# One fixed order on TensorE for the matmuls and transposes of a layer's expert pairs

## Chip, core and metric

The kernel runs on one core of a Trainium2 chip. The metric is device time in microseconds (us). The median of three runs before the change is 1332.66 us (1327.23 to 1333.02); the profile below is of a further execution, which took 1326.95 us.

## What is computed

The reference is one step of a two-layer backbone over 512 latent tokens and 128 context tokens of width 1024. Each layer mixes tokens (attention, pooling, convolution) and then sends them through 16 experts. The expert part, which the change touches, is:

```
aff = softmax(u @ w_router)                  # per token, over 16 experts
g, idx = top_k(aff.T, cap)                   # cap = 64 latent tokens or 16 context tokens per expert
xs = u[idx]
hdn = silu(xs @ w_gate) * (xs @ w_up)        # 1024 -> 512
ye = (hdn @ w_down) * g                      # 512 -> 1024
out = zeros.at[idx].add(ye)
x = layer_norm(ALPHA * x + gate2 * out)
```

All of it is float32. The weights of one expert are 6 MB, so a layer reads 96 MB of them.

## The kernel before

`experts` runs the 16 experts as eight pairs, j = 0 to 7, in a loop that Python unrolls. The two experts of a pair share the 128 columns of TensorE: `lat` (L1129) computes gate and up for the latent rows with expert i in columns 64i to 64i+63, and `context` (L1137) does the same for the context rows with four products (two experts, gate and up) in 32 columns each. `lat_down` (L1187) and `ctx_down` (L1159) are the down projections, in two tiles of 64 columns and four of 32. `lat(0)` and `lat(1)` are the two halves of the contraction over 1024, `context(ks)` any of its eight steps k.

One f32 matmul leaves two MATMUL records in the profile, so a pair has 64 records of `ps_g` and `ps_u`, 64 of `ps_gc`, 32 of `ps_d` and 32 of `ps_dc`. Records on different column tiles that start together are called a round here: four records of a 32-column product or two of a 64-column product. A pair is thus 32 + 16 + 16 + 8 = 72 rounds. To these come 16 transposes: eight in `load_x` (via `transpose8`, L239), which turn the gathered rows of the next pair, four of `hT` (L1176, `lat_transpose`) and four of `hcT` (L1152, in `ctx_down`).

Between them stand the other engines. `lat_hidden` makes h = silu(ps_g) * ps_u (ScalarE L1167, VectorE L1169); `ctx_down` makes hc alike from `ps_gc` (L1145, L1147) and copies `ps_hcT` out (L1153); `lat_transpose` copies `ps_hT` out in two halves (L1177, L1178); `modulate` (L247, L250) scales each of `load_x`'s eight transposed blocks into `xT`, four to a PSUM bank, by turns on VectorE and ScalarE. GpSimd gathers the rows of the next pair (L947) and scatters the results into DRAM with two indirect DMAs each (L1094: `yacc` for latent rows, `yaccc` for context rows). SyncE issues the weight loads (L1062), twelve of 1 MB per pair, into 16 slots; a load into a slot waits until the matmuls that read the slot's last tile are done.

PSUM: `ptr` gives out two banks (`tr8`, `ps_hT`, and before the change `ps_hcT`), `pmisc` one, `ps_gu` three (`ps_g`, `ps_u`, `ps_gc`), `ps_dn` two (`ps_d`, `ps_dc`).

What decides the order: the program's order is a priority only. A list scheduler simulates the engines while the kernel is built and gives each engine the instruction that its model holds ready; a fixed edge between two instructions exists only where data or `tc.issue_after` makes one. So the order on TensorE of `lat`, `context`, `ctx_down` and the next pair's first matmuls, which depend on one another little, is what the model picks. Before the change the program's order for pairs 1 to 6 is `context(0..3)`, `lat(0)`, `lat(1)`, `context(4..7)`, hT, `load_x`, `lat_down`, `ctx_down`. Pair 0 fills the routing's waits with `context`. After pair 7 `join` adds the residual and the last pair's results in PSUM (`ps_z`, L1261 to L1266) and `finish` normalises each block of 128 tokens.

Of the kernel before, what the change touches and what calls it, by code (L numbers as in the profile page):

```python
# [21 lines left out]
P = 128  # L22
D = 1024
TL = 512
# [3 lines left out]
KD = 8  # L28
# [16 lines left out]
NPAIR = NE // 2  # L45
# [20 lines left out]
def kernel(ctx: ExitStack, tc: tile.TileContext, a: dict):  # L66
# [44 lines left out]
    def ptr(name):  # L111
        return ps_t.tile([P, 512], F32, tag="tr", name=name)
# [118 lines left out]
        nc.tensor.matmul(out, lhsT=lh, rhs=rl, start=False, stop=False)  # L231
        nc.tensor.matmul(out, lhsT=ll, rhs=rh, start=False, stop=last)  # L232

    def transpose8(src, emit, psum=ptr):

        for g in range(2):
            ps = psum("tr8").rearrange("p (k n) -> p k n", k=4)
            for kk in range(4):
                ins = nc.tensor.transpose(ps[:, kk, :], src[:, 512 * g + kk:512 * g + 512:4], ident)  # L239
            emit(g, ps)  # L240
        return ins

# [799 lines left out]
    def experts(l, A, B, ctxr, ln, gates, newrow, newhalf, residual, xc, route_late, ps_dn, preload, start_next, finish, keep):  # L1042
        wk = opool(f"moe{l}", "right")
        ex = [opool(f"exp{i}_{l}", "right") for i in range(NEX)]
        ps_gu = Banks(f"gu{l}", 3)
        nslot, paced = [0], []

        def eload(src, shape, name):

# [34 lines left out]
        def load_x(j):  # L1084
            x = gather(newrow("xsl"), zrow[:, :], lgi[:, j:j + 1]) if j else x_first
            xT = xp.tile([P, KD, P], F32, tag="xT", name="xT", bufs=2)
            transpose8(x, lambda g, ps: modulate(xT[:, 4 * g:4 * g + 4], ps, A, B, 0, g))
            return xT

        def scatter(acc, y, idx, j):  # L1090
# [15 lines left out]
        for j in range(NPAIR):  # L1106
# [18 lines left out]
            def lat(hf):  # L1125
                for ps, nm in ((pg, "g"), (pu, "u")):
                    for k in range(4 * hf, 4 * hf + 4):
                        for i in range(2):
                            nc.tensor.matmul(ps[64 * i:64 * i + 64, :], lhsT=xT[:, k, 64 * i:64 * i + 64],  # L1129
                                             rhs=w[nm, i, hf][:, k % 4, :], start=(k == 0), stop=(k == KD - 1))  # L1130

            def context(ks):

                for k in ks:
                    for q in range(4):
                        i, nm = q // 2, "gu"[q % 2]
                        ins = nc.tensor.matmul(pc[32 * q:32 * q + 32, :], lhsT=xc[:, k, 16 * es[i]:16 * es[i] + 32],  # L1137
                                               rhs=w[nm, i, k // 4][:, k % 4, :], start=(k == 0), stop=(k == KD - 1))
                return ins

            def ctx_down(pd=None, after=None):
                sc = newhalf("sc")
                hc = newhalf("hc")[0:64]
                for i in range(2):
                    nc.scalar.activation(out=sc[64 * i + 32:64 * i + 64], in_=pc[64 * i:64 * i + 32], func=AF.Silu)  # L1145
                    with tc.issue_after(after.ins) if after else ExitStack():
                        nc.vector.tensor_tensor(out=hc[32 * i:32 * i + 32], in0=pc[64 * i + 32:64 * i + 64],  # L1147
                                                in1=sc[64 * i + 32:64 * i + 64], op=ALU.mult)
                hcT = wk.tile([P, 4, 64], F32, tag="hcT", name="hcT", bufs=1)
                pt = ptr("ps_hcT")[:, 0:256].rearrange("p (k n) -> p k n", k=4)  # L1150
                for k in range(4):
                    nc.tensor.transpose(pt[:, k, :], hc[:, 256 * (k // 2) + k % 2:256 * (k // 2) + 256:2], ident[0:64, 0:64])  # L1152
                nc.scalar.copy(out=hcT, in_=pt)  # L1153
                if pd is None:
                    pd = ps_dn.tile("ps_dc")
                for f in range(4):
                    for q in range(4):
                        i, n = q // 2, q % 2
                        nc.tensor.matmul(pd[32 * q:32 * q + 32, :], lhsT=hcT[:, f, 32 * i:32 * i + 32],  # L1159
                                         rhs=w["d", i, f // 2][:, f % 2, n * 512:n * 512 + 512], start=(f == 0), stop=(f == 3))  # L1160
                yc = newhalf("yc") if j == NPAIR - 1 else wk.tile([P, 512], F32, tag="yc", name="yc", bufs=2)
                nc.vector.scalar_tensor_tensor(out=yc, in0=pd, scalar=cg[:, j:j + 1], in1=gc2, op0=ALU.mult, op1=ALU.mult)  # L1162
                return yc

            def lat_hidden():
                sg = newhalf("sg")
                nc.scalar.activation(out=sg, in_=pg, func=AF.Silu)  # L1167
                h = newhalf("h")
                nc.vector.tensor_tensor(out=h, in0=pu, in1=sg, op=ALU.mult)  # L1169
                return h  # L1170

            def lat_transpose(h):
                hT = wk.tile([P, 4, P], F32, tag="hT", name="hT", bufs=1)
                pt = ptr("ps_hT").rearrange("p (k n) -> p k n", k=4)
                for k in range(4):
                    nc.tensor.transpose(pt[:, k, :], h[:, 256 * (k // 2) + k % 2:256 * (k // 2) + 256:2], ident)  # L1176
                nc.scalar.copy(out=hT[:, 0:2], in_=pt[:, 0:2])  # L1177
                nc.vector.tensor_copy(out=hT[:, 2:4], in_=pt[:, 2:4])  # L1178
                return hT

            def lat_down(hT):
                ye = newrow("ye")
                for n in range(2):
                    pd = ps_dn.tile("ps_d")
                    for f in range(4):
                        for i in range(2):
                            nc.tensor.matmul(pd[64 * i:64 * i + 64, :], lhsT=hT[:, f, 64 * i:64 * i + 64],  # L1187
                                             rhs=w["d", i, f // 2][:, f % 2, n * 512:n * 512 + 512], start=(f == 0), stop=(f == 3))
                    hs = slice(n * 512, n * 512 + 512)
                    order["ye"] = nc.vector.scalar_tensor_tensor(out=ye[:, hs], in0=pd, scalar=lg[:, j:j + 1], in1=gl2[:, hs], op0=ALU.mult, op1=ALU.mult)  # L1190
                return ye

            if j == 0:
                quads = list(range(KD))

                def fill(n, after=None):
                    ks = [quads.pop(0) for _ in range(min(n, len(quads)))]
                    with tc.issue_after(after.ins) if after else ExitStack():
                        return context(ks)

                (lgi, lso, lg, llast), x_first = route_late(fill)
                xp = opool(f"xT{l}", "left")
                scatter(yaccc, ctx_down(after=order["lgi"]), csi, j)
                x_next = load_x(0)
                for t in (1, 2, 3):
                    residual(t, order["last"].ins if t == 3 else None)
            xT = x_next
            if j == 0:
                lat(0)
                lat(1)  # L1210
            elif j < NPAIR - 1:
                context(range(4))
                lat(0)
                lat(1)
                context(range(4, 8))
            else:
                lat(0)
                lat(1)
                context(range(4))
            hT = lat_transpose(lat_hidden())  # L1220
            if j < NPAIR - 1:
                x_next = load_x(j + 1)
            ye = lat_down(hT)
            if j == MIDAT:
                order["mid"] = order["ye"]
            if j < NPAIR - 1:
                scatter(yacc, ye, lso, j)
                if j:
                    scatter(yaccc, ctx_down(), csi, j)


        z2 = []
# [6 lines left out]
                                    scalar2=None, op0=ALU.is_equal)  # L1239
        hotr = newhalf("hotr", F32R)  # L1240
        nc.vector.tensor_scalar(out=hotr, in0=iota, scalar1=llast[:, 0:1], scalar2=None, op0=ALU.is_equal)
        context(range(4, 8))
        yh, yl = gates.tile([P, D], F32R, tag="gate", name="yh"), newrow("yl", dt=F32R)
        for n in range(2):
            cols = slice(n * 512, n * 512 + 512)
# [9 lines left out]

        def join(t):
            res = []
            for n in range(2):
                ps = seats(t, n)
                cols = slice(n * 512, n * 512 + 512)  # L1260
                nc.tensor.matmul(ps, lhsT=ident, rhs=zs[t][:, cols], start=True, stop=False)  # L1261
                if t == CTX:
                    nc.tensor.matmul(ps, lhsT=hot[:, TL + n * P:TL + (n + 1) * P], rhs=yc, start=False, stop=True)
                else:
                    for y in (yh, yl):
                        nc.tensor.matmul(ps, lhsT=hotr[:, t * P:(t + 1) * P], rhs=y[:, cols], start=False, stop=y is yl)  # L1266
# [244 lines left out]
```

## Time and profile before

| | |
|---|---|
| median of three runs | 1332.66 us |
| the profiled execution | 1326.95 us, its span 1325.1 us |
| TensorE (PE) busy | 1237.7 us, 93% of the span |
| VectorE, ScalarE, GpSimd busy | 542.6, 370.7, 253.7 us |
| chain of work that ended last | PE 86%, DVE 7%, ACT 3%, DMA 2% |
| moved by DMA | 342.35 MB, 258 GB/s over the span |

The profile has one line per group of instructions or per stretch of time. PE is TensorE, DVE VectorE, ACT ScalarE, POOL GpSimd, SPq the queue of SyncE. PEclk is the granted share of TensorE's clock: 1.00 is the upper of its two levels (2.4 GHz). `L1129` is the line of the kernel; `ps_g<-wg,xT 128*64` is a matmul into `ps_g` from `wg` and `xT` on a tile of 128 rows and 64 columns. The chain of waits is read back from the last instruction: each piece is what the next one waited for.

### The profile page before, as it was taken

How to read it: one execution, taken by the hardware profiler on the slowest of the kernel's cores; microseconds unless marked ns; L12 is line 12 of the kernel's file. 1: busy time of each engine (PE TensorE's matmuls, PEld its weight loads, DVE VectorE, ACT ScalarE, POOL GpSimd, SP SyncE). 2: the span in 40 equal slices, each digit the busy share in tenths (PEclk: the TensorE clock that was granted, in tenths of full speed). 3: DMA queues.
4: the chain of work that ended last, by engine and by line, in shares of the span. 5: the costliest groups of instructions: out<-in, count | busy, mean ns of one | idle time of the engine just before them, and what ended most of it. 6: DMA issues, size and time to landing. Idle time of an engine off the chain costs nothing.

```text
span 1325.1 us, 18215 instructions
## 1 busy us (share of the span) xinstructions
PE 1237.7 (93%) x7244; PEld 716.4 (54%) x7244; DVE 542.6 (41%) x1266; ACT 370.7 (28%) x800; POOL 253.7 (19%) x234
## 2 busy tenths in 40 slices
PE   4999999999699999999978999999968999999994
PEld 1877786977333333233248998798743333333322
DVE  1554365776611121112196666577662111111216
ACT  1532145752321111011144423475341111101111
POOL 1210002005221220122166100200523122012204
PEclk8999999999899999999988999999999999999997
DMA  9868657065799999998442214606479999999831
GB/s 357 306 223 281 235 210 276 2 225 190 277 381 407 395 398 420 361 320 282 147 135 96 74 54 193 249 5 224 168 293 350 406 397 397 421 370 328 299 100 79
DMA packets 85078, 342.35 MB, mean 258 GB/s; under 512 B 18712, under 2 KB 32088, under 8 KB 54400
## 3 DMA queue, kind: packets, MB, share of 16 engines
q1 hardware_dynamic: 73568, 305.96, 59.5%
q0 software_dynamic: 9840, 29.45, 8.6%
q10 hardware_dynamic: 1584, 5.77, 1.1%
q8 instruction: 57, 0.93, 0.3%
q14 instruction: 29, 0.24, 0.1%
HBM read 313.73 MB, written 27.51 MB: 258 GB/s over the span
## 4 chain that ended last, share of the span: by engine, by line
PE 86%; DVE 7%; ACT 3%; DMA 2%; issue 1%; POOL 0%; SPq 0%; POOLq 0%; ACTq 0%; DVEq 0%
PE ps_gc L1137 10%; PE ps_d L1187 9%; PE ps_u L1129 9%; PE ps_g L1129 9%; PE ps_dc L1159 5%; PE ps_ada L185 4%; PE ps_c L230 3%; PE ps_c L232 3%; PE ps_c L231 3%; PE ps_o L231 3%; PE ps_o L230 3%; PE ps_o L232 3%; PE tr L239 2%; DMA r_wA<-in_w_in_dram 1%; PE ps_p L719 1%; PE ps_a L232 1%
## 5 line engine op out<-in xcount | busy, mean ns | idle before, releaser
L1129 PE MATMUL ps_u<-wu,xT 128*64 128x512 f32 x512 | 134.9, 595 | 0.0
L1137 PE MATMUL ps_gc<-wu,xc 128*32 128x512 f32 x512 | 134.0, 596 | 0.0
L1137 PE MATMUL ps_gc<-wg,xc 128*32 128x512 f32 x512 | 132.9, 596 | 0.0
L1129 PE MATMUL ps_g<-wg,xT 128*64 128x512 f32 x512 | 131.8, 597 | 0.1
L1187 PE MATMUL ps_d<-wd,hT 128*64 128x512 f32 x512 | 122.9, 598 | 3.5 <-ACT hT L1177 3.1
L1169 DVE TENSOR_TENSOR h<-ps_u,sg 128x512 f32<-128x512 f32 x16 | 11.1, 691 | 239.3 <-PE ps_u L1129 212.5
L1129 PEld LDWEIGHTS ps_u<-wu,xT 128*64 128x64 f32 x512 | 40.2, 137 | 82.4 <-issue 77.0
L1094 POOL DMA_INDIRECT yaccc<-yc,csi x28 | 39.8, 1423 | 216.6 <-DVE yc L1162 155.1
L1129 PEld LDWEIGHTS ps_g<-wg,xT 128*64 128x64 f32 x512 | 37.7, 136 | 79.7 <-issue 71.4
L1167 ACT ACTIVATE sg<-ps_g 128x512 f32<-128x512 f32 x16 | 9.5, 596 | 252.7 <-PE ps_g L1129 252.7
L1187 PEld LDWEIGHTS ps_d<-wd,hT 128*64 128x64 f32 x512 | 35.8, 136 | 70.0 <-issue 62.2
L1159 PE MATMUL ps_dc<-wd,hcT 128*32 128x512 f32 x512 | 67.3, 620 | 0.9 <-ACT hcT L1153 0.9
L185 PE MATMUL ps_ada<-wada,cs 128*32 128x512 f32 x368 | 58.8, 615 | 6.0 <-DMA wada<-in_w_ada_dram 6.0
L1137 PEld LDWEIGHTS ps_gc<-wg,xc 128*32 128x32 f32 x512 | 29.2, 109 | 51.7 <-issue 49.1
L1145 ACT ACTIVATE sc<-ps_gc 32x512 f32<-32x512 f32 x32 | 18.8, 588 | 129.5 <-PE ps_gc L1137 106.2
L247 ACT ACTIVATE xT<-tr,modB,modA 128x128 f32<-128x128 f32 x64 | 29.1, 458 | 85.7 <-DVE xT L250 85.3
L1162 DVE SCALAR_TENSOR_TENSOR yc<-ps_dc,cg,gc 128x512 f32<-128x512 f32 x16 | 12.0, 751 | 95.5 <-PE ps_dc L1159 85.4
L1137 PEld LDWEIGHTS ps_gc<-wu,xc 128*32 128x32 f32 x512 | 30.3, 109 | 37.4 <-issue 35.8
L250 DVE TENSOR_SCALAR xT<-tr,modA,modB 128x128 f32<-128x128 f32 x64 | 26.0, 408 | 57.0 <-PE tr L239 49.3
L947 POOL DMA_INDIRECT xsl<-zrow,lgi x16 | 15.9, 992 | 160.4 <-PE tr L239 146.1
L1190 DVE SCALAR_TENSOR_TENSOR ye<-ps_d,lg,gl 128x512 f32<-128x512 f32 x32 | 23.8, 749 | 48.5 <-PE ps_d L1187 48.5
L1147 DVE TENSOR_TENSOR hc<-ps_gc,sc 32x512 f32<-32x512 f32 x32 | 22.0, 688 | 50.9 <-ACT sc L1145 50.6
(610 smaller groups left out, 2824.4 us busy)
## 6 DMA issues: line engine op xcount, KB each, us to landing
wg<-in_w_gate_dram SPq DMA_DIRECT2D x64, 1024.0 KB, 11.4
wu<-in_w_up_dram SPq DMA_DIRECT2D x64, 1024.0 KB, 13.2
wd<-in_w_down_dram SPq DMA_DIRECT2D x64, 1024.0 KB, 14.7
wada<-in_w_ada_dram SPq DMA_DIRECT2D x46, 1024.0 KB, 7.0
r_wo<-in_w_out_dram SPq DMA_DIRECT2D x8, 1024.0 KB, 8.6
zrow<-xa ACTq DMA_DIRECT2D x8, 512.0 KB, 8.4
yacc<-xa POOLq DMA_DIRECT2D x8, 512.0 KB, 8.9
z<-yacc SPq DMA_DIRECT2D x8, 512.0 KB, 8.4
```

The source lines that it names most:

```text
L185: nc.tensor.matmul(ps[32 * j:32 * j + 32, :], lhsT=cs[:, k, :], rhs=w[:, j * 512:(j + 1) * 512], start=(k == 0), stop=(k == KD - 1))
L230: nc.tensor.matmul(out, lhsT=lh, rhs=rh, start=first, stop=False)
L231: nc.tensor.matmul(out, lhsT=lh, rhs=rl, start=False, stop=False)
L232: nc.tensor.matmul(out, lhsT=ll, rhs=rh, start=False, stop=last)
L239: ins = nc.tensor.transpose(ps[:, kk, :], src[:, 512 * g + kk:512 * g + 512:4], ident)
L247: nc.scalar.activation(out=out[:, kk, :], in_=ps[:, kk, :], func=AF.Identity, scale=A[:, r, k:k + 1], bias=B[:, r, k:k + 1])
L250: nc.vector.tensor_scalar(out=out[:, kk, :], in0=ps[:, kk, :], scalar1=A[:, r, k:k + 1], scalar2=B[:, r, k:k + 1], op0=ALU.mult, op1=ALU.add)
L1094: nc.gpsimd.indirect_dma_start(out=acc[:, :], out_offset=bass.IndirectOffsetOnAxis(ap=idx[h][0:64, j:j + 1], axis=0), in_=y[hs], in_offset ...
L1129: nc.tensor.matmul(ps[64 * i:64 * i + 64, :], lhsT=xT[:, k, 64 * i:64 * i + 64], rhs=w[nm, i, hf][:, k % 4, :], start=(k == 0), stop=(k == ...
L1137: ins = nc.tensor.matmul(pc[32 * q:32 * q + 32, :], lhsT=xc[:, k, 16 * es[i]:16 * es[i] + 32], rhs=w[nm, i, k // 4][:, k % 4, :], start=(k ...
L1159: nc.tensor.matmul(pd[32 * q:32 * q + 32, :], lhsT=hcT[:, f, 32 * i:32 * i + 32], rhs=w["d", i, f // 2][:, f % 2, n * 512:n * 512 + 512], ...
L1187: nc.tensor.matmul(pd[64 * i:64 * i + 64, :], lhsT=hT[:, f, 64 * i:64 * i + 64], rhs=w["d", i, f // 2][:, f % 2, n * 512:n * 512 + 512], s ...
```

## The change

A helper `inline` gives every matmul and transpose made through `mm` or `turn1` an edge behind the one made before it, without a semaphore, so that within a layer's expert part TensorE runs them in the program's order. The program's order for pairs 1 to 6 becomes `lat(0)`, `context` whole, hc, `lat(1)`, h, `load_x`, the transposes of hc, those of h, the context rows' down projection, `lat_down`. Pair 0 has `load_x(1)` ahead of hT. Pair 7 keeps three of its eight `context` steps for behind `lat_down` and has one between hT and `lat_down`. `ps_hcT` moves from the two `ptr` banks to the `pmisc` bank. The matmuls of the first two joins are in the line, the last pair's `ps_hcT` and `ps_dc` behind them. Nothing that is computed changes.

```diff
+    line = {}
+
+    def inline(op, *args, **kw):
+
+        with tc.issue_after(line["pe"].ins) if line else ExitStack():
+            line["pe"] = op(*args, **kw)
+        return line["pe"]
+
+    def mm(*args, **kw):
+        return inline(nc.tensor.matmul, *args, **kw)
+
+    def turn1(*args):
+        return inline(nc.tensor.transpose, *args)
+
-    def transpose8(src, emit, psum=ptr):
+    def transpose8(src, emit, psum=ptr, turn=nc.tensor.transpose):
...
         def load_x(j):
             x = gather(newrow("xsl"), zrow[:, :], lgi[:, j:j + 1]) if j else x_first
             xT = xp.tile([P, KD, P], F32, tag="xT", name="xT", bufs=2)
-            transpose8(x, lambda g, ps: modulate(xT[:, 4 * g:4 * g + 4], ps, A, B, 0, g))
+            transpose8(x, lambda g, ps: modulate(xT[:, 4 * g:4 * g + 4], ps, A, B, 0, g),
+                       turn=turn1 if j else nc.tensor.transpose)
...
-            def ctx_down(pd=None, after=None):
+            def ctx_hidden(after=None):
                 sc = newhalf("sc")
...
+                return hc
+
+            def ctx_turn(hc):
                 hcT = wk.tile([P, 4, 64], F32, tag="hcT", name="hcT", bufs=1)
-                pt = ptr("ps_hcT")[:, 0:256].rearrange("p (k n) -> p k n", k=4)
+                pt = pmisc("ps_hcT")[:, 0:256].rearrange("p (k n) -> p k n", k=4)
...
+            def ctx_rows(hcT, pd=None):
...
-                scatter(yaccc, ctx_down(after=order["lgi"]), csi, j)
-                x_next = load_x(0)
+                scatter(yaccc, ctx_rows(ctx_turn(ctx_hidden(order["lgi"]))), csi, j)
+                xT = load_x(0)
...
-            xT = x_next
-            if j == 0:
                 lat(0)
                 lat(1)
+                h = lat_hidden()
+                x_next = load_x(j + 1)
+                hT = lat_transpose(h)
             elif j < NPAIR - 1:
-                context(range(4))
                 lat(0)
+                context(range(KD))
+                hc = ctx_hidden()
                 lat(1)
-                context(range(4, 8))
+                h = lat_hidden()
+                x_next = load_x(j + 1)
+                hcT = ctx_turn(hc)
+                hT = lat_transpose(h)
+                scatter(yaccc, ctx_rows(hcT), csi, j)
             else:
                 lat(0)
                 lat(1)
+                h = lat_hidden()
                 context(range(4))
-            hT = lat_transpose(lat_hidden())
-            if j < NPAIR - 1:
-                x_next = load_x(j + 1)
+                hT = lat_transpose(h)
+                context(range(4, 5))
             ye = lat_down(hT)
...
             if j < NPAIR - 1:
                 scatter(yacc, ye, lso, j)
-                if j:
-                    scatter(yaccc, ctx_down(), csi, j)
...
-        context(range(4, 8))
+        context(range(5, KD))
...
         joined = [join(t) for t in range(2)]
-        yc = ctx_down(pmisc("ps_dc"))
+        hcT = ctx_turn(ctx_hidden())
+        yc = ctx_rows(hcT, pmisc("ps_dc"))
```

The matmuls of `lat`, `context`, the down projections and the joins t = 0 and 1 are now made through `mm`, the transposes of h and hc through `turn1`.

## Rows read from the trace of the kernel before

**Rows 1.** The page: busy time of the engines, share of the span, instructions.
```profile
PE 1237.7 (93%) x7244; PEld 716.4 (54%) x7244; DVE 542.6 (41%) x1266; ACT 370.7 (28%) x800; POOL 253.7 (19%) x234
```
**Rows 2.** Stretches, first layer: us, PE busy (instructions), PEclk, DMA share, GB/s.
```profile
418.55:452.79 34.24, 34.16 (x212) 1.00 1.02 405
...
524.04:563.32 39.28, 39.23 (x212) 1.00 0.95 370
563.32:605.20 41.88, 41.35 (x212) 1.00 0.93 329
...
sum 273.89, PE 272.15; mean PE 34.02
```
**Rows 3.** The same stretches, second layer.
```profile
sum 271.92, PE 270.15; mean PE 33.77
```
**Rows 4.** Chain of waits, 418.5 to 454: start us, us, what.
```profile
433.69 3.43 PE ps_dc L1159 x32
...
445.86 3.43 PE ps_u L1129 x16
449.29 3.67 PE ps_gc L1137 x32
```
**Rows 5.** Chain of waits, 563 to 606.
```profile
573.85 0.98 PE ps_gc L1137 x2
...
595.18 0.98 PE ps_gc L1137 x2
596.15 1.00 PE ps_u L1129 x2
```
**Rows 6.** PE in order of time: start, us, line, records [idle before, releaser].
```profile
606.40 7.09 PE L1187 MATMUL ps_d<-wd,hT 128*64 128x512 f32 x32 [0.46 <-ACT hT L1177]
613.42 1.24 PE L239 MATMUL tr<-ident,xsl 128*128 128x128 f32 x8
...
429.43 0.69 PE L1152 MATMUL ps_hcT<-ident,hc 64*128 64x64 f32 x4
452.79 0.74 PE L1176 MATMUL ps_hT<-ident,h 128*128 128x128 f32 x4
```
**Rows 7.** VectorE and ScalarE in order of time: h, then one bank of xT.
```profile
415.16 0.69 DVE L1169 TENSOR_TENSOR h<-ps_u,sg 128x512 f32<-128x512 f32 x1 [14.18 <-PE ps_u L1129]
...
393.22 0.41 DVE L250 TENSOR_SCALAR xT<-tr,modA,modB 128x128 f32<-128x128 f32 x1 [3.65 <-PE tr L239]
...
394.60 0.46 ACT L247 ACTIVATE xT<-tr,modB,modA 128x128 f32<-128x128 f32 x1 [0.48 <-DVE xT L250]
```
**Rows 8.** Around the first join of the last layer, PE and VectorE in order of time.
```profile
1290.32 1.12 PE L1261 MATMUL ps_z<-z,ident 128*128 128x512 f32 x2
1297.46 1.02 PE L1261 MATMUL ps_z<-z,ident 128*128 128x512 f32 x2
...
1291.11 1.28 DVE L227 TENSOR_TENSOR yl<-ye,yh 128x512 fp32r<-128x512 f32 x2
```
**Rows 9.** DMA between 386 and 645: all, the gate loads' landing, one issue.
```profile
DMA packets 15347, 93.08 MB, mean 359 GB/s; under 512 B 1840, under 2 KB 2545, under 8 KB 5297
...
wg<-in_w_gate_dram SPq DMA_DIRECT2D x24, 1024.0 KB, 10.3
...
543.13 0.83 SPq L1062 DMA_DIRECT2D wg<-in_w_gate_dram  x2
```
**Rows 10.** What TensorE waited for ahead of L1129: us in total, times.
```profile
  DMA wu<-in_w_up_dram: 4.5, 6
```
**Rows 11.** GpSimd in order of time (gathers and scatters); the gather's landing, 386 to 645.
```profile
401.26 1.45 POOL L1094 DMA_INDIRECT yacc<-ye,lgi  x1 [16.25 <-DVE ye L1190]
409.31 1.41 POOL L1094 DMA_INDIRECT yacc<-ye,lso  x1 [6.60 <-DMA yacc<-ye,lgi]
572.26 0.98 POOL L947 DMA_INDIRECT xsl<-zrow,lgi  x1 [29.45 <-PE tr L239]
...
xsl<-zrow,lgi POOLq DMA_INDIRECT x5, 11.0
```

More of the change, by code (lines that the diff above doesn't have):

```diff
@@ L238, in transpose8 @@
             for kk in range(4):
-                ins = nc.tensor.transpose(ps[:, kk, :], src[:, 512 * g + kk:512 * g + 512:4], ident)
+                ins = turn(ps[:, kk, :], src[:, 512 * g + kk:512 * g + 512:4], ident)
             emit(g, ps)
@@ L1046, in experts @@
         nslot, paced = [0], []
+        line.clear()
         def eload(src, shape, name):
@@ L1128, in lat @@
                         for i in range(2):
-                            nc.tensor.matmul(ps[64 * i:64 * i + 64, :], lhsT=xT[:, k, 64 * i:64 * i + 64],
-                                             rhs=w[nm, i, hf][:, k % 4, :], start=(k == 0), stop=(k == KD - 1))
+                            mm(ps[64 * i:64 * i + 64, :], lhsT=xT[:, k, 64 * i:64 * i + 64],
+                               rhs=w[nm, i, hf][:, k % 4, :], start=(k == 0), stop=(k == KD - 1))
             def context(ks):
@@ L1136, in context @@
                         i, nm = q // 2, "gu"[q % 2]
-                        ins = nc.tensor.matmul(pc[32 * q:32 * q + 32, :], lhsT=xc[:, k, 16 * es[i]:16 * es[i] + 32],
-                                               rhs=w[nm, i, k // 4][:, k % 4, :], start=(k == 0), stop=(k == KD - 1))
+                        ins = mm(pc[32 * q:32 * q + 32, :], lhsT=xc[:, k, 16 * es[i]:16 * es[i] + 32],
+                                 rhs=w[nm, i, k // 4][:, k % 4, :], start=(k == 0), stop=(k == KD - 1))
                 return ins
-            def ctx_down(pd=None, after=None):
+            def ctx_hidden(after=None):
                 sc = newhalf("sc")
@@ L1148, in ctx_down @@
                                                 in1=sc[64 * i + 32:64 * i + 64], op=ALU.mult)
+                return hc
+            def ctx_turn(hc):
                 hcT = wk.tile([P, 4, 64], F32, tag="hcT", name="hcT", bufs=1)
-                pt = ptr("ps_hcT")[:, 0:256].rearrange("p (k n) -> p k n", k=4)
+                pt = pmisc("ps_hcT")[:, 0:256].rearrange("p (k n) -> p k n", k=4)
                 for k in range(4):
-                    nc.tensor.transpose(pt[:, k, :], hc[:, 256 * (k // 2) + k % 2:256 * (k // 2) + 256:2], ident[0:64, 0:64])
+                    turn1(pt[:, k, :], hc[:, 256 * (k // 2) + k % 2:256 * (k // 2) + 256:2], ident[0:64, 0:64])
                 nc.scalar.copy(out=hcT, in_=pt)
+                return hcT
+            def ctx_rows(hcT, pd=None):
                 if pd is None:
@@ L1158, in ctx_down @@
                         i, n = q // 2, q % 2
-                        nc.tensor.matmul(pd[32 * q:32 * q + 32, :], lhsT=hcT[:, f, 32 * i:32 * i + 32],
-                                         rhs=w["d", i, f // 2][:, f % 2, n * 512:n * 512 + 512], start=(f == 0), stop=(f == 3))
+                        mm(pd[32 * q:32 * q + 32, :], lhsT=hcT[:, f, 32 * i:32 * i + 32],
+                           rhs=w["d", i, f // 2][:, f % 2, n * 512:n * 512 + 512], start=(f == 0), stop=(f == 3))
                 yc = newhalf("yc") if j == NPAIR - 1 else wk.tile([P, 512], F32, tag="yc", name="yc", bufs=2)
@@ L1175, in lat_transpose @@
                 for k in range(4):
-                    nc.tensor.transpose(pt[:, k, :], h[:, 256 * (k // 2) + k % 2:256 * (k // 2) + 256:2], ident)
+                    turn1(pt[:, k, :], h[:, 256 * (k // 2) + k % 2:256 * (k // 2) + 256:2], ident)
                 nc.scalar.copy(out=hT[:, 0:2], in_=pt[:, 0:2])
@@ L1186, in lat_down @@
                         for i in range(2):
-                            nc.tensor.matmul(pd[64 * i:64 * i + 64, :], lhsT=hT[:, f, 64 * i:64 * i + 64],
-                                             rhs=w["d", i, f // 2][:, f % 2, n * 512:n * 512 + 512], start=(f == 0), stop=(f == 3))
+                            mm(pd[64 * i:64 * i + 64, :], lhsT=hT[:, f, 64 * i:64 * i + 64],
+                               rhs=w["d", i, f // 2][:, f % 2, n * 512:n * 512 + 512], start=(f == 0), stop=(f == 3))
                     hs = slice(n * 512, n * 512 + 512)
@@ L1191, in lat_down @@
                 return ye
+            if j:
+                xT = x_next
             if j == 0:
@@ L1257, in join @@
             res = []
+            put = mm if t < 2 else nc.tensor.matmul
             for n in range(2):
@@ L1260, in join @@
                 cols = slice(n * 512, n * 512 + 512)
-                nc.tensor.matmul(ps, lhsT=ident, rhs=zs[t][:, cols], start=True, stop=False)
+                put(ps, lhsT=ident, rhs=zs[t][:, cols], start=True, stop=False)
                 if t == CTX:
-                    nc.tensor.matmul(ps, lhsT=hot[:, TL + n * P:TL + (n + 1) * P], rhs=yc, start=False, stop=True)
+                    put(ps, lhsT=hot[:, TL + n * P:TL + (n + 1) * P], rhs=yc, start=False, stop=True)
                 else:
                     for y in (yh, yl):
-                        nc.tensor.matmul(ps, lhsT=hotr[:, t * P:(t + 1) * P], rhs=y[:, cols], start=False, stop=y is yl)
+                        put(ps, lhsT=hotr[:, t * P:(t + 1) * P], rhs=y[:, cols], start=False, stop=y is yl)
                 res.append(ps)
```

## The prediction

> **What bounds the kernel now.** I read the page first: TensorE is busy for 93% of the span and no other engine for half of it [rows 1], and the chain of waits is 86% TensorE. So the question is not who waits for whom but whether a busy TensorE does full work. I then cut the two expert parts at the first transpose of h of each pair. Each stretch holds the same work, 208 records and a few of a neighbour's, at the same full clock, and TensorE has hardly a gap in any. Yet the second takes 34.24 us, the fifth 39.28 and the sixth 41.88 [rows 2]. From the first cut to the first join it is 273.89 us in layer 0 and 271.92 in layer 1 [rows 2, 3].
>
> The chain of waits shows why. In the 34.24 us stretch the pieces are whole: 32 records of `ps_dc` in 3.43 us, eight rounds of four, and 16 of `ps_u` in 3.43 us, eight rounds of two [rows 4]. A round is 0.429 us whether it holds two or four records. In the 41.88 us stretch the pieces are chopped: two records of `ps_gc`, a quarter of two rounds, take 0.98 us, and two of `ps_u`, half of two rounds, 1.00 us [rows 5]. A lone matmul costs two whole rounds (its two records share a tile) with the other tiles empty, and about 0.12 us for the change of tile shape. That is the loss.
>
> **What the order gives.** The program's order has k outside and the column tiles inside, so an unbroken line makes only whole rounds. A new pair (1 to 6) from these rows:
> - 72 rounds of 0.429 us: 30.9 us;
> - eight transposes of gathered rows 1.2, four of hc 0.6, four of h 0.6 [rows 6]: 2.4 us;
> - six changes of tile shape. Eight rounds of `ps_gc` that end in one take 3.67 us against 3.43, of which about 0.1 is the last record's own tail [rows 4]; 0.14 each: 0.8 us.
>
> Together 34.1 us, and the clean stretch with the same rounds and transposes is 34.24, which bears the sum out.
>
> **What it adds: a wait for a PSUM bank.** `load_x` now stands ahead of hT and takes both `ptr` banks; hT can have the first again when `modulate` has read it. VectorE does h first (0.69 us, begun some 0.2 us behind the last `ps_u`), then four operations on the bank run by turns on VectorE and ScalarE, from 393.22 to 394.60 + 0.46: 1.84 us [rows 7]. So the bank is free some 2.85 us behind `lat(1)`. TensorE has 1.2 + 0.6 us of transposes until then (`ps_hcT` has a bank of its own) and waits 1.05 us; the line keeps it from doing anything else. Below, this is 0 where the builder's model puts the four operations ahead of h and they end in time; above, 2.5 us where ScalarE works off all eight operations before it copies hcT, for which the down projection waits. I take 1.05, since the rows give each part of it. The copies of hT (0.46 us where nothing covers them [rows 6]) lie beside the 3.4 us of `ps_dc`. New pair: 35.15 us; six are 210.9.
>
> Pair 0 from the first cut: 1.95 us to the bank, hT 0.6, its copy 0.5, down projection 7.0 [rows 6]: 10.05. Pair 7 up to the first join: 32 rounds of `lat` 13.7, ten of `context` 4.3 (eight hide h, two hide hT's copy), hT 0.6, 16 rounds down 6.9, six of `context` 2.6, five shape changes 0.7: 28.8. The sum is 249.7 us per layer, 24.2 and 22.2 less than now.
>
> **The end of a layer.** The last pair's hcT and `ps_dc` (0.6 + 0.5 + 3.5 us) come behind the first two joins instead of ahead of them, so the third join, now at 7.1 us after the first [rows 8], comes up to 4.6 us later. Against that the split of ye (1.28 us on VectorE, now ahead of the first join's end [rows 8]) hides beside six rounds of `context`, while hc's two multiplications, each of h's size, move into VectorE's busy tail. From there VectorE and GpSimd set the end, not TensorE. Bounds: nothing to 4.6 us a layer; I take 1.5, nearer to nothing because VectorE has two blocks to normalise meanwhile.
>
> **Moved things at no cost.** The scatter of yc (two indirect DMAs on GpSimd) now goes ahead of that of ye; both feed sums read at the layer's end. The gather of the next rows keeps its place ahead of the pair's scatters. SyncE's loads keep their order; the slots of `wd` are freed earlier, since both down projections stand together. The first joins' line changes nothing, as that is their order now. If the cover of the weights went, TensorE would wait: next part.
>
> **Sum.** 24.2 + 22.2 − 3.0 = 43.4 us. The profiled execution took 1326.95 us (span 1325.1, 1.85 around it), which gives 1283.5; the median of the runs is 5.7 us above that execution. I forecast against the mean of the four, 1330: **1287 us**.
>
> **Rivals.**
> 1. *The DMA becomes the bound* (0.06). For: its share is 1.02 in the clean stretch, at 405 GB/s, so 13.9 MB a pair, which alone is 34.2 us [rows 2]. Against: from 386 to 645 the DMA moves 93.08 MB [rows 9], 230 us at 405 GB/s, and the last weights are wanted some 240 us in; and weights come early: pair 6's first gate loads, issued at 543.13, landed in some 10.3 us (the median) [rows 9] and were first read at 573.85 [rows 5]. If the rate fell to 370 GB/s [rows 2], the 230 became 252, 12 us a layer more than wanted: 1311 us. The Trainium skill, Perfetto Trace Analysis, section Roofline, gives about 435 GB/s as what 16 DMA engines move in all; by it the 93.08 MB would take 214 us, an estimate, and the trace's 405 lies below it.
> 2. *A late gather holds the line; slower than before* (0.04). A fixed order can't work around rows that aren't there. A gather lands 11.0 us after its issue, and a pair's two scatters to `yacc` hold GpSimd from 401.26 to 409.31 + 1.41, 9.5 us, since the second waits for the first [rows 11]. If GpSimd did both scatter pairs of j−1 ahead of the gather, it would land 19 + 11 = 30 us into the pair, and the line wants it at 21, behind 48 rounds: 9 us, twelve times, 108 us, so 1395. It decides from 3.6 us a pair (43.4 / 12). Against it: the gather issued at 572.26 is read at 613.42 [rows 11, 6], a pair ahead.
> 3. *The chopped rounds cost nothing that order could save* (0.04): they fill waits for weights, which would show as gaps in a fixed order. TensorE's waits ahead of `lat` for up weights are 4.5 us in all [rows 10], and pair 6's were long there, so little speaks for it. Time: 1330. The Trainium skill, TensorEngine Tiling (Array Packing), section Key Properties, says that tiles operate independently and different tiles can run matmuls in parallel; if that held across a broken round, the empty tiles would be filled by what follows and the gain would be nil. The trace disagrees: two records on one tile took 0.98 us.
>
> **How the numbers follow.** The forecast has 0.86. Its range: without the bank waits (14 × 1.05 = 14.7) and with nothing at the layers' ends (3), 1269; with 2.5 us a wait (+20.3) and 4.6 us at each end (+6.2), 1314, which takes in the first rival. Range 1269 to 1314. A measurement of this kernel tells about 0.5% from no change, 6.7 us. Faster takes the forecast and the first rival, 0.92; same 0.04; slower 0.04.
>
> **What would show it.** After: stretches of pairs 1 to 6 all alike, 34 to 36 us, at some 208 records; pieces of 16 and 32 records alone in the chain; TensorE idle about 1 us ahead of `ps_hT`, released by xT; SyncE waiting for `ps_d` where it waited for `ps_dc`; the tail behind the first join as long as now or a few us longer. Wrong if pairs lengthen towards the layer's end, if TensorE waits for `wg`, `wu` or `xsl`, or if the wait for the bank is over 2 us.

## The result, and the profile after

The changed kernel takes **1295.3 us** (median of four runs, 1293.7 to 1299.3) beside 1332.8 for the kernel before (four runs, 1327.2 to 1333.0): ratio 0.973, 95% interval 0.970 to 0.977. It is faster by 37.5 us; the forecast was 1287 (43.4 us faster), the range 1269 to 1314. The profiled execution of the changed kernel took 1294.5 us, its span 1292.7, so between the two traces 32.4 us of span are to be found. (The traced execution of before lies 5.8 us under its median, the traced one of after 0.8 under its own.)

The page of the kernel after, busy times, TensorE's granted clock in 40 slices, and the chain by engine:

```profile
PE 1193.2 (92%) x7244; PEld 710.7 (55%) x7244; DVE 543.7 (42%) x1266; ACT 368.3 (28%) x800; POOL 252.8 (20%) x234
...
PEclk8999999999979999999989999999998999999998
...
PE 84%; DVE 7%; ACT 4%; DMA 2%; issue 1%; SPq 1%; POOL 0%; POOLq 0%; ACTq 0%; DVEq 0%
```

The same 7244 TensorE instructions are busy for 1193.2 us instead of 1237.7 [rows 1]. No work has gone; the same records lie more closely together. TensorE is still the bound.

The stretches, now from the end of `lat(1)` of pair 0 to the first join (the first cut of [rows 2, 3] is the start of hT, which the change moves). Columns: us, PE busy, PEclk, DMA share, GB/s. First the kernel before:

```profile
385.80:660.60 274.80, 272.17 (x1494) 1.00 0.92 347
1017.50:1290.32 272.82, 270.16 (x1494) 1.00 0.91 344
```

The kernel after: the two stretches, then what follows each of them (first join of layer 0 to the end of `lat(1)` of pair 0 in layer 1; first join of layer 1 to the end):

```profile
386.11:642.14 256.03, 246.77 (x1459) 0.98 0.98 374
997.47:1255.38 257.91, 247.08 (x1459) 0.98 0.95 365
642.14:997.47 355.33, 326.62 (x2040) 0.97 0.45 160
1255.38:1292.74 37.36, 19.13 (x80) 0.84 0.18 71
```

The stretches lost 18.8 and 14.9 us (the last pair's `ps_hcT` and `ps_dc`, some 36 records, now stand behind the first joins and so outside, as the forecast had it). Before, 356.9 us lay between them (660.60 to 1017.50) and 34.8 behind the second (1290.32 to the end at 1325.1): the first became 1.6 shorter, the last 2.5 longer. With 0.3 us more ahead of the first stretch this is the 32.4 us.

The pairs of the kernel after, cut at hT, five of the twelve, same columns:

```profile
420.95:456.19 35.24, 34.01 (x209) 1.00 1.02 400
...
491.42:528.29 36.87, 35.65 (x208) 0.95 1.02 408
528.29:565.26 36.97, 35.71 (x208) 0.95 1.02 409
565.26:600.50 35.24, 34.01 (x208) 1.00 1.02 367
...
1067.55:1104.48 36.93, 35.71 (x208) 0.95 1.02 401
```

No pair lengthens towards the end of the layer, as pairs did in [rows 2]. But there are two kinds: 35.24 us, which is the 35.15 of the sum, and some 36.9 us, with 1.7 us more of busy time at a lower granted clock. Where that sits is read from the chain of waits of the kernel after, 488 to 505 (start us, us, what):

```profile
488.41 1.17 PE tr L239 x8
489.58 0.63 PE ps_hcT L239 x4
...
490.29 0.37 ACT hcT L1172
490.66 0.72 ACT xT L261 x2
...
491.42 0.82 PE ps_hT L239 x4
492.25 5.13 PE ps_dc L239 x32
...
504.39 3.43 PE ps_g L239 x16
```

(All matmuls in the line have the helper's line, L239.) Every piece is whole: 16 of `ps_g` in 3.43 us, as `ps_u` in [rows 4], none of two records as in [rows 5]. `ps_dc` alone has 5.13 us for the eight rounds that took 3.43 in [rows 4] and take 3.57, with a change of tile shape, in the pairs of 35.24 us (at 456.93, for one). The stretch of `ps_dc` by itself, all engines' busy time, then PEclk 0.69:

```profile
492.17:497.30 5.13, 5.13 (x33) 1.15 (x32) 0.42 (x1) 0.37 (x1) 0.00 (x0) 0.69 1.01 423
```

The trace's record of the granted clock has it at 0.5 (1.2 GHz) for 3.41 us from 491.95 on, and again from 529.50, 601.17, 1068.80, 1140.48 and 1178.03: six of the twelve pairs. Each time it falls between the last 0.3 us of hT's transposes and 0.7 us into `ps_dc`. A pair with a drop takes some 36.9 us against 35.24, so each costs 1.7 us, some 10 us in all. Before, the 16 transposes of a pair didn't stand together. In the stretch of 34.24 us [rows 2] they were in three groups with matmul rounds between, the third being hcT at 429.43 [rows 6]:

```profile
418.55 0.74 PE L1176 MATMUL ps_hT<-ident,h 128*128 128x128 f32 x4
419.13 0.65 PE L239 MATMUL tr<-ident,xsl 128*128 128x128 f32 x4
...
425.17 0.75 PE L239 MATMUL tr<-ident,xsl 128*128 128x128 f32 x4
```

The clock was 1.00 in these stretches [rows 2].

TensorE's longest wait in the kernel after, 385 to 643 (us in total, times, longest):

```profile
PE ps_hT L239 <- ACT xT L261: 8.8, 7, 1.5
```

In layer 1, 996 to 1256, the same wait has the same 8.8 us, and behind it comes one that the sum didn't have, in pair 6:

```profile
PE ps_d L239 <- DVE yc L1184: 1.6, 1, 1.6
```

There VectorE made ye ahead of yc, and the second half of `ps_d` had to wait for the bank that yc is read from.

And the longest of SyncE's queue, 386 to 640:

```profile
SPq L1077 <- PE ps_d L239: 66.4, 12, 13.5
```

The bank wait is there, released by `xT` as foretold: 1.23 us in six pairs, 1.5 in pair 0. SyncE now waits for `ps_d`. There is no wait for `wg`, `wu` or `xsl` in TensorE's list of either layer.

### The profile page after: what moved, and what is told of

Same layout as the page of the kernel before. It is cut to its first block, busy times and chain, and to the rows that moved or that the text cites. A ratio compares the mean times of both kernels' runs of the same rounds, so it can differ in the third digit from the quotient of the medians.

```text
span 1292.7 us, 18180 instructions
## 1 busy us (share of the span) xinstructions
PE 1193.2 (92%) x7244; PEld 710.7 (55%) x7244; DVE 543.7 (42%) x1266; ACT 368.3 (28%) x800; POOL 252.8 (20%) x234
## 4 chain that ended last, share of the span: by engine, by line
PE 84%; DVE 7%; ACT 4%; DMA 2%; issue 1%; SPq 1%; POOL 0%; POOLq 0%; ACTq 0%; DVEq 0%
PE ps_d L239 9%; PE ps_g L239 9%; PE ps_u L239 9%; PE ps_gc L239 8%; PE ps_dc L239 5%; PE ps_ada L185 4%; PE ps_c L230 3%; PE ps_c L232 3%; PE ps_c L231 3%; PE ps_o L231 3%; PE ps_o L230 3%; PE ps_o L232 3%; PE ps_p L733 1%; PE tr L239 1%; PE ps_b L230 1%
## 5 line engine op out<-in xcount | busy, mean ns | idle before, releaser
L239 PE MATMUL ps_g<-wg,xT 128*64 128x512 f32 x512 | 116.1, 595 | 0.1
L239 PE MATMUL ps_d<-wd,hT 128*64 128x512 f32 x512 | 113.6, 595 | 2.5 <-DVE yc L1184 1.6
L239 PE MATMUL ps_u<-wu,xT 128*64 128x512 f32 x512 | 115.4, 592 | 0.0
L239 PE MATMUL ps_gc<-wu,xc 128*32 128x512 f32 x512 | 115.0, 595 | 0.0
L239 PE MATMUL ps_gc<-wg,xc 128*32 128x512 f32 x512 | 115.0, 594 | 0.0
L1161 ACT ACTIVATE sc<-ps_gc 32x512 f32<-32x512 f32 x32 | 18.8, 587 | 328.8 <-PE ps_gc L239 299.7
L239 PEld LDWEIGHTS ps_d<-wd,hT 128*64 128x64 f32 x512 | 35.5, 137 | 78.7 <-issue 75.7
L239 PEld LDWEIGHTS ps_g<-wg,xT 128*64 128x64 f32 x512 | 36.0, 137 | 75.1 <-issue 72.7
L239 PEld LDWEIGHTS ps_u<-wu,xT 128*64 128x64 f32 x512 | 37.2, 137 | 72.6 <-issue 71.8
L239 PE MATMUL ps_dc<-wd,hcT 128*32 128x512 f32 x512 | 71.1, 705 | 0.9 <-ACT hcT L1172 0.9
L239 PEld LDWEIGHTS ps_gc<-wg,xc 128*32 128x32 f32 x512 | 29.2, 110 | 75.0 <-issue 73.7
L239 PEld LDWEIGHTS ps_dc<-wd,hcT 128*32 128x32 f32 x512 | 17.2, 126 | 43.0 <-issue 39.1
L285 POOL TENSOR_TENSOR bsd<-bsd,neg_half 128x1 f32<-128x1 f32 x15 | 9.5, 634 | 128.7 <-DVE bsd L284 128.7
L227 POOL TENSOR_TENSOR wo00l<-r_wo,wo00h 128x1024 fp32r<-128x1024 f32 x4 | 10.4, 2610 | 119.4 <-ACT wo00h L226 119.4
## 6 DMA issues: line engine op xcount, KB each, us to landing
wu<-in_w_up_dram SPq DMA_DIRECT2D x64, 1024.0 KB, 14.9
```

Of the source, the lines that this page charges most:

```text
L239: line["pe"] = op(*args, **kw)
```

## Experiments

"The line" is the fixed order that the helper makes. The theory: the line is worth what the broken rounds cost; the change gives back part of it in the wait for hT's bank and, behind that wait, in the clock. Rivals: the program's new order did it, not the line; the clock falls where the DMA is busiest, whatever TensorE did; the tail of a layer took what is missing.

### hT in a bank of its own

`ps_gc`'s bank has long been read when hT is transposed. The edit takes away what hT waits for:

```diff
 def lat_transpose(h):
-    pt = ptr("ps_hT").rearrange("p (k n) -> p k n", k=4)
+    pt = (ptr("ps_hT") if j == NPAIR - 1 else pc).rearrange("p (k n) -> p k n", k=4)
```

> Edit of the changed kernel: hT is transposed into the PSUM bank of its own pair's context product (free since hc was made) instead of one of the two banks that the gathered rows' transposes hold; the line is the same. Theory: the wait for the bank (1.23 us, 14 times, 17 us) goes, and with it the six drops of the granted clock to 0.5 behind it (1.7 us each, 10 us), less up to 0.7 us a pair for the copy of hcT, late now: 1268 to 1277 us. Rival: the clock drops come from the run of 16 transposes as such, and stay: 1278 to 1287 us.

1268.2 us (1266.9 to 1268.8, four runs), ratio 0.953, interval 0.950 to 0.956: 27 us below the change. Two of its pairs (us, PE busy, PEclk, DMA share, GB/s):

```profile
454.59:488.53 33.94, 33.94 (x209) 1.00 1.02 406
...
522.48:556.42 33.94, 33.94 (x210) 1.00 1.02 409
```

TensorE's longest waits, 383 to 660:

```profile
PE ps_d L239 <- DVE yc L1184: 1.6, 1, 1.6
PE ps_d L239 <- ACT hT L1199: 0.8, 1, 0.8
```

Busy time is now all of the stretch, the wait for `xT` has gone, and no pair of either layer has the lower clock. The sum of the two is 17.6 us (14 waits) and some 10 (six drops), nearly 28; 27 came back. (The wait of `ps_d` for yc, which the changed kernel has in layer 1 alone, is now in both layers.) The DMA share is 1.02 and still no weight is waited for. This is the best version that was run.

### The line taken out

```diff
 def inline(op, *args, **kw):
-    with tc.issue_after(line["pe"].ins) if line else ExitStack():
-        line["pe"] = op(*args, **kw)
-    return line["pe"]
+    return op(*args, **kw)
```

> Edit of the changed kernel: the helper makes no edge any more; program order, banks and pair 7's split stay as changed. Theory (the line is what makes whole rounds): the list scheduler chops rounds again, later pairs take 37 us and more, 1310 to 1335 us. Rival (the new program order is enough): pairs stay within 36 us, 1285 to 1300 us.

1323.6 us (six runs), ratio 0.994, interval 0.992 to 0.996. Two stretches of it, cut at hT:

```profile
535.47:576.56 41.09, 40.28 (x216) 1.00 1.02 405
576.56:618.22 41.66, 40.61 (x209) 1.00 0.78 257
```

Pieces of its chain of waits, 576 to 618:

```profile
575.66 0.98 PE ps_gc L238 x2
...
584.91 0.98 PE ps_gc L238 x4
```

The late pairs are as long as in [rows 2] and the pieces of 0.98 us of [rows 5] are back. The rest of the change without the line (order, banks and pair 7's split, not taken apart here) is worth some 8 us; the program's order is a priority that the builder's model overrides.

### The line alone, on the old order and the old banks

The kernel before, its matmuls and transposes made through `inline` and nothing else changed:

```diff
-                            nc.tensor.matmul(ps[64 * i:64 * i + 64, :], lhsT=xT[:, k, 64 * i:64 * i + 64],
+                            mm(ps[64 * i:64 * i + 64, :], lhsT=xT[:, k, 64 * i:64 * i + 64],
...
-                    nc.tensor.transpose(pt[:, k, :], h[:, 256 * (k // 2) + k % 2:256 * (k // 2) + 256:2], ident)
+                    turn1(pt[:, k, :], h[:, 256 * (k // 2) + k % 2:256 * (k // 2) + 256:2], ident)
...
```

> Edit of the kernel before: only the line is added, with that kernel's own program order and banks (hT ahead of the gathered rows' transposes, context rows' down projection last). Theory (whole rounds are the gain, and the new program order costs a bank wait): pairs of 34.2 us plus about 0.8 us of waits for copies, no clock drops, 1278 to 1292 us. Rival (the new program order is part of the gain, for the old one makes the line wait for h, hcT or weights): pairs over 36 us, 1300 us or more.

1288.4 us (1286.3 to 1291.1, four runs), ratio 0.968, interval 0.965 to 0.971. A pair of it (all twelve are between 35.71 and 35.77):

```profile
457.03:492.77 35.74, 34.07 (x212) 1.00 1.02 410
```

TensorE's longest waits, 383 to 660:

```profile
PE tr L239 <- DVE hT L1193: 7.4, 7, 1.2
PE ps_dc L239 <- ACT hcT L1168: 3.0, 6, 0.5
```

So the line gives 43 us by itself, and the rest of the change takes some 7 back. The old order in a line waits even longer in a pair (1.2 for hT's copy, 0.5 for hcT's; 35.74 us against 35.24), yet none of the twelve drops in clock: its transposes and waits stand in other places, with rounds between them, and the longest piece without one is 3.1 us, against 3.7 in the changed kernel. So a wait of 1.2 us by itself does not bring the drop. (Pair 0 of layer 0 drops once; there the piece is 4 us long.)

### A longer wait for hcT

`ps_hcT` back in the two `ptr` banks, in the new order:

```diff
-                pt = pmisc("ps_hcT")[:, 0:256].rearrange("p (k n) -> p k n", k=4)
+                pt = ptr("ps_hcT")[:, 0:256].rearrange("p (k n) -> p k n", k=4)
```

> Edit of the changed kernel: ps_hcT goes back to the two banks that ps_hT and the gathered rows share. Theory: hcT now takes the first bank that modulate frees and hT has to wait for the second, so TensorE waits 2.9 to 3.2 us in a pair instead of 1.23, 20 to 24 us in all, and the granted clock drops in most of the twelve pairs instead of six (up to 10 us more): 1315 to 1330 us. Rival (the drops have nothing to do with the wait): six drops or so as now, 1314 to 1319 us, or no more waiting at all where the scheduler finds another order on VectorE, 1295 us.

1299.3 us (1297.8 to 1302.2, four runs), ratio 0.977, interval 0.974 to 0.980. TensorE's longest wait, 383 to 660:

```profile
PE ps_hcT L239 <- ACT xT L261: 8.8, 6, 1.5
```

Two of its pairs:

```profile
456.36:493.53 37.17, 35.71 (x209) 0.95 1.02 400
...
530.71:566.19 35.48, 34.01 (x209) 1.00 1.02 398
```

The expected wait of about 3 us did not come, and the time is under both expectations of a longer one: hcT waits 1.5 us and hT then finds its bank free, so there is one wait a pair as before, 0.24 us longer. The median is 4 us above the change, with runs that overlap; the traces are clearer. From pair 0's hT to pair 7's the layers take 245.1 and 246.7 us, 3.2 and 2.9 more than in the change. Twelve longer waits are 2.9 of that; the rest is three more drops in clock (eight of the twelve and pair 0 once, against six), less the 1.6 us wait for yc, which does not occur. The transposes and the wait are together 4.0 us here.

### hT behind the context rows' down projection

The wait's length shares a place with the transposes; this one keeps them all, but puts the eight rounds of `ps_dc` between hcT and hT in pairs 1 to 6:

```diff
                 hcT = ctx_turn(hc)
-                hT = lat_transpose(h)
                 scatter(yaccc, ctx_rows(hcT), csi, j)
+                hT = lat_transpose(h)
```

> Edit of the changed kernel: in pairs 1 to 6 hT's four transposes come behind the context rows' down projection instead of ahead of it; banks and line as changed. TensorE then waits about 0.5 us for the copy of hcT and 0.5 for that of hT instead of 1.23 for the bank, and the stretch without matmul rounds is cut in two. Theory (the clock falls behind the long stretch of transposes and wait): no drops in pairs 1 to 6, 10 us, and 0.2 us a pair: 1280 to 1288 us. Rival (it falls wherever TensorE waits about 1 us in a pair): drops stay, 1291 to 1297 us.

1287.3 us (1281.9 to 1289.8, four runs), ratio 0.967, interval 0.963 to 0.971. A pair of it:

```profile
496.32:531.43 35.11, 34.08 (x212) 1.00 1.02 406
```

TensorE's longest waits, 383 to 660:

```profile
PE ps_d L239 <- ACT hT L1199: 3.6, 7, 0.5
PE ps_dc L239 <- ACT hcT L1172: 3.0, 6, 0.5
```

Waits are still 1.0 us a pair, but in two pieces with matmul rounds between, and the clock is 1.00 in pairs 1 to 6 of both layers. (Pair 0 is as it was in the change; in layer 1 its clock drops.) The DMA moves as many GB/s as in the change's own pairs, so a heavy DMA does not make the drop. Side by side, the longest piece of transposes and waits without a matmul round, and the drops in twelve pairs: 2.5 us, none (hT in its own bank); 3.1, none (the line alone); 3.7, six (the change); 4.0, eight (hcT in `ptr`). So the drop goes with the length of this piece, and cutting the piece in two took the drops out of pairs 1 to 6. The length doesn't settle it for one pair: pair 0 of the changed kernel has a piece of 3.9 us and dropped in neither layer, and the run of the next section, where its code is the same, dropped there in both. Which pairs are hit, and why six and not twelve, stays open.

### Broken rounds priced by themselves

In pair 3 alone the context steps run tile by tile, with k inside: the same matmuls, no round of four left.

```diff
-                for k in ks:
-                    for q in range(4):
+                for k, q in [(k, q) for q in range(4) for k in ks] if j == 3 else [(k, q) for k in ks for q in range(4)]:
+                    if True:
```

> Edit of the changed kernel: in pair 3 of both layers the context product runs through all eight steps k of one column tile before the next tile, instead of all four tiles at each k; the same 32 matmuls. Theory (a tile whose neighbours get no work leaves them empty): its 16 rounds become 61 to 64, 45 to 48 more at 0.429 us, 19 to 21 us a layer, 1333 to 1338 us. Rival (tiles run independently of the order): nothing changes, 1293 to 1299 us.

1326.2 us in one run, beside 1332.3 for before on the same chip and 1295.3 for the change: 31 of the 37 us gained are undone by one pair in eight. That pair's stretch in layer 0:

```profile
459.83:510.58 50.75, 49.52 (x208) 1.00 0.87 332
```

TensorE in order of time at the boundary of the first two tiles (start, us, records):

```profile
477.95 5.77 PE L239 MATMUL ps_gc<-wg,xc 128*32 128x512 f32 x13
483.13 0.62 PE L239 MATMUL ps_gc<-wu,xc 128*32 128x512 f32 x1
483.56 0.59 PE L239 MATMUL ps_gc<-wg,xc 128*32 128x512 f32 x1
483.59 0.59 PE L239 MATMUL ps_gc<-wu,xc 128*32 128x512 f32 x1
```

50.75 against 35.24 is 15.5 us, not the 19 to 21 of 64 lone rounds: 64 records at 0.429 us, less 12, are 52 rounds, 36 more than 16, 15.4 us. (In layer 1 the stretch is 52.45 us, with a drop in clock in it.) The 12 are the three boundaries: the next tile's first four records (`wu` at the first boundary) start beside the last four of the tile before (`wg`). So tiles do overlap across a broken round, but only some four records deep. The third rival's rule holds in part: it saves 12 of the 48 rounds that a tile by itself would add, a quarter.

The Trainium skill, TensorE: Matmul & The Clock Gate, Part 3, The mechanism, says that matmuls start and end strictly in the order of the program. These rows differ: in the program all 16 `wg` records of the tile stand ahead of the first `wu`, yet that one starts at 483.13 and a `wg` at 483.56.

### A late gather

The gather of the next rows put behind the last scatter of the pair before, which is the second rival's case made on purpose:

```diff
         def load_x(j):
-            x = gather(newrow("xsl"), zrow[:, :], lgi[:, j:j + 1]) if j else x_first
+            with tc.issue_after(order["sc"].ins) if j else ExitStack():
+                x = gather(newrow("xsl"), zrow[:, :], lgi[:, j:j + 1]) if j else x_first
...
-                nc.gpsimd.indirect_dma_start(out=acc[:, :], out_offset=bass.IndirectOffsetOnAxis(ap=idx[h][0:64, j:j + 1], axis=0),
+                order["sc"] = nc.gpsimd.indirect_dma_start(out=acc[:, :], out_offset=bass.IndirectOffsetOnAxis(ap=idx[h][0:64, j:j + 1], axis=0),
```

> Edit of the changed kernel: each gather of a next pair's rows gets an edge behind the last scatter of the pair before, so GpSimd can't run ahead. By the prediction's second rival it lands some 30 us into the pair and TensorE waits 9 us, twelve times: about 1395 us. By the scatters of the changed kernel's trace, which are issued some 11 us into the next pair, it lands at 20 to 24 us where 21 is wanted: 0 to 3 us a pair, 1295 to 1330 us.

1342.8 us in one run, beside 1332.3 (nine runs, 1326.8 to 1333.5): slower than before, as far as one run tells. TensorE's longest wait, 383 to 680:

```profile
PE tr L239 <- DMA xsl<-zrow,lgi: 15.7, 6, 5.0
```

GpSimd in order of time, the gather behind the scatter:

```profile
415.22 1.41 POOL L1111 DMA_INDIRECT yacc<-ye,lso  x1 [7.14 <-DMA yacc<-ye,lgi]
416.93 0.98 POOL L961 DMA_INDIRECT xsl<-zrow,lgi  x1 [0.30 <-issue]
```

The wait is 2.6 us a pair in the mean, not the rival's 9, and 31 us in both layers, but the time went up by 47 us over the change: the mean granted clock of the whole run fell to 0.947 (0.966 in the change), and its drops follow the longer halts ahead of the transposes. In this line a late operand cost its wait and then the clock behind it.

### The end of a layer, twice

Both undo the moved tail in the version with hT's own bank (1268.2 us), so that the tail is told from the pairs. First only the order of the joins:

```diff
+        hcT = ctx_turn(ctx_hidden())
+        yc = ctx_rows(hcT, pmisc("ps_dc"))
         joined = [join(t) for t in range(2)]
-        hcT = ctx_turn(ctx_hidden())
-        yc = ctx_rows(hcT, pmisc("ps_dc"))
```

> Edit of e1_own_bank: the last pair's hcT and context down projection stand ahead of the first two joins, as before the change, instead of behind them. Theory (behind the joins they are hidden beside VectorE, but make the end 2.5 us longer): the joins start 4.6 us later and the end is 2.5 us shorter, in each layer, so 1.5 to 4.5 us slower than e1_own_bank, 1270 to 1273 us. Rival (the longer end costs more than it hides): 1264 to 1267 us.

1285.6 us (five runs), ratio 0.966, interval 0.964 to 0.969; 17 us more, outside both expectations. TensorE's two longest waits from 600 to 700:

```profile
PE tr L253 <- ACT umod L261: 6.9, 1, 6.9
PE ps_hcT L239 <- DVE hc L1163: 5.1, 1, 5.1
```

hc comes late since its steps 5 to 7 stand behind `lat_down`, and ScalarE has the casts of two tiles of the next layer's weights between its two halves; so this isn't the old tail. The second version has all eight context steps ahead of hT and hc at once:

```diff
                 h = lat_hidden()
-                context(range(4))
+                context(range(KD))
+                hc = ctx_hidden()
                 hT = lat_transpose(h)
-                context(range(4, 5))
...
-        context(range(5, KD))
...
+        hcT = ctx_turn(hc)
+        yc = ctx_rows(hcT, pmisc("ps_dc"))
         joined = [join(t) for t in range(2)]
-        hcT = ctx_turn(ctx_hidden())
-        yc = ctx_rows(hcT, pmisc("ps_dc"))
```

> The version with hT in its own bank, with the end of a layer undone in full: pair 7 computes all eight context steps ahead of hT, makes hc at once, and its hcT and ps_dc stand ahead of the first two joins instead of behind them; no context steps are kept to fill the wait for the split of ye. My theory (moving them behind the joins takes them off the path to the first join, but puts them on the path to the third; what is left is small): 1269 to 1276 us, 0.5 to 4 us a layer more than the 1268.2 of that version, most of it as TensorE waiting ahead of the first join and ahead of ps_d in pair 7. Rival (the moved tail brings nothing, or costs what I had put it at, 1.5 us a layer): 1264 to 1268 us. If it comes out well over 1280, something other than the order (ScalarE's queue, as in the first try) holds hcT again.

1282.5 us (1279.2 to 1282.9, four runs), ratio 0.963, interval 0.960 to 0.966. TensorE in order of time, pair 7 of layer 0:

```profile
629.80 10.02 PE L239 MATMUL ps_d<-wd,hT 128*64 128x512 f32 x32 [6.77 <-ACT hT L1199]
```

ScalarE at the same place:

```profile
627.92 1.56 ACT L226 CAST wA10h<-r_wA 128x768 fp32r<-128x768 f32 x2 [4.91 <-DMA r_wA<-in_w_in_dram]
629.39 0.36 ACT L1199 COPY hT<-ps_hT 128x256 f32<-128x256 f32 x1
```

ScalarE took the casts of the next layer's weights ahead of the copy of hT and waited 4.9 us for their load; TensorE, held by the line, waited 6.8 us and then ran `ps_d` in 10.0 us instead of 7.1, at a mean granted clock of 0.70. Layer 1 has no next layer and no such casts. The stretch from its last hT to the end, in this kernel:

```profile
1231.96:1281.10 49.14, 28.56 (x116) 0.86 0.20 82
```

And in the version with hT's own bank:

```profile
1218.07:1266.84 48.77, 30.53 (x148) 0.85 0.28 110
```

The latter has eight rounds (3.4 us) of context still to do in it. So the undone tail is 49.14 − (48.77 − 3.4) = 3.8 us longer in layer 1, in one trace of each. There the moved tail is a gain, not a cost; what it is worth in layer 0 is mixed up with ScalarE's order and isn't settled.

## Why the prediction was right, and where its sum was off

**What bounds the kernel** held: the loss was in broken rounds of a TensorE that was busy throughout. Line and order taken apart show it (old order 1332, with the line 1288; new order 1324, with the line 1295), and so does the price: 0.429 us a round explains pair 3 of layer 0 run tile by tile to 0.1 us once the overlap at the tiles' boundaries is counted.

**The pair** held where the clock did: 35.24 us against 35.15. The bank wait was 1.23 us, not 1.05. Its pieces, 0.2, 0.69 and 1.84 us, add up to 2.73 and not to the 2.85 that was written, and ScalarE copies hcT (0.37 us) ahead of its last scalings of the bank, a part of what the upper bound of 2.5 was made of. The sign "all alike, 34 to 36 us" did not hold for half of the pairs.

**The term that was missing** is TensorE's clock, and with it the sum of the stretches fell short. "Six are 210.9" took the full clock for granted, as it was in all stretches of before [rows 2]. The change puts twelve transposes, a wait and four more transposes in one piece, and in half the pairs the clock granted behind it is 0.5 for 3.4 us. The stretches gave 33.7 us, not 46.4, each counted from the end of `lat(1)`. The 12.7 are some 10.1 of clock (six drops), 1.6 of the wait of `ps_d` for yc, which the sum did not have either, and 1.0 of twelve pairs at 35.24 for 35.15; pairs 0 and 7 came out within 0.1. That 1295 lay in the range is in part luck: the room above the forecast was made for bank waits of up to 2.5 us and longer ends, and the clock used it.

**The end of a layer** was put at +1.5 each and came out at −1.6 and +2.5, +0.9 in all; the first is below the bound of nothing. The mechanism was seen one-sidedly: in layer 1 the undone tail costs 3.8 us. Behind the joins `ps_dc` also gets out of the way of what VectorE needs first, and the context steps kept back cover the copy of hT; which of the two brings the gain was not taken apart.

**Moved things at no cost** held for the loads and gathers: no wait for weights or gathered rows, SyncE's queue waiting for `ps_d`. With both down projections together, though, `ps_d` waited once for the bank of `ps_dc`, the 1.6 us above; the kernel before has no such wait.

**The rivals.** The DMA did not become the bound: 95.70 MB between 386 and 642 are 374 GB/s in the mean, and even at 33.94 us a pair, with a share of 1.02, no weight is waited for. There may be little left below that, though: the 13.9 MB of a pair are 34 us at the 409 GB/s of its second row, an estimate. The late gather did not occur, but its mechanism is real: made on purpose, it ended slower than before in its one run. The third rival fell with the line's 43 us, though its rule holds for some four records.

The 8.3 us between forecast and median are the 11.0 by which the sum missed the traces (32.4 for 43.4), less the 3.1 between the traced execution of before and the 1330 that the forecast started from, and some 0.4 besides.

## What to carry to other kernels

A busy engine can be half empty: compare stretches of equal work, and where a list scheduler mixes column tiles of several shapes, fix the order of whole rounds with edges that need no semaphore. Having fixed it, look at every operand in the line once more, since nothing can step into a gap: give what comes last a bank of its own, and keep a few rounds back to cover a copy. And price a gap on TensorE at its length plus what the clock may lose behind it; here that was 1.7 us on a wait of 1.23, in the pairs that it hit. Putting matmul rounds between two groups of transposes avoided it and took 8 us off the time.

## What the runs showed of the hardware

- Transposes did not keep the clock up here. The piece at which each drop begins is 3.7 us long; TensorE was busy with transposes for 2.5 of it and idle for 1.23 only, and the granted clock still fell to 0.5 for 3.4 us in six pairs of twelve. With a wait of 1.2 us and a piece of 3.1 it did not fall in any.
- Matmuls of one tile shape on another column tile started ahead of up to three records that stand before them in the program, so that four of the next tile's ran beside the last four of the tile before; beyond that the other tiles stood empty (52 rounds for 64 records on one tile after the other).
- Of two versions, the one with the longer waits in a pair (1.7 us against 1.23) was the faster: its pairs are 35.74 us throughout, the other's 35.24 or 36.9.
